# Writing the low parts of weight tiles in pieces of 256 columns on GpSimd

## The chip, the cores and the metric

The kernel runs on one core of one Trainium2 chip. The metric is the device time of one execution in microseconds; smaller is better. The engines are named as in the profile: PE is TensorE (PEld its weight loads), DVE is VectorE, ACT is ScalarE, POOL is GpSimd, SP is SyncE, which issues nearly all DMAs.

## The reference

One layer of a streaming encoder and a final norm, on x of 1024 positions by 1024 channels, all in float32:

```
h = rmsnorm(x) ; proj = h @ w_in          # 4 blocks for a gated DeltaNet, 3 for band attention, 2 branch gates
oa = gated_delta_rule(silu(conv(q)), silu(conv(k)), silu(conv(v)), g, beta)   # 4 heads of 128, chunks of 64
oa = rmsnorm(oa) * silu(z)
ob = chunk_band_attention(qb, kb, vb, rel_bias)                               # 8 heads of 64, band of 9 chunks
mix = sigmoid(ga) * (oa @ w_branch_a) + sigmoid(gb) * (ob @ w_branch_b)
x = x + mix @ w_out
h = rmsnorm(x) ; u = causal_dwconv3(h @ w_up) + b ; gate, up = split(u)
x = x + (silu(gate) * up) @ w_down
return rmsnorm(x)
```

## The kernel before, in words

Every large product is made of three products of a rounded type, float32r, so that float32 accuracy is nearly kept: each operand a is split into a high part `hi` (a rounded copy, made by ACT) and a low part `lo = a - hi` (made by POOL or DVE), and PE adds hi·hi, hi·lo and lo·hi. The function `split` (line 80) issues that pair of instructions; its argument `eng` names the engine of the subtraction, and POOL is taken when it is left out.

`load_w` (line 84) fetches one weight tile of 128 x nk x 128 numbers (nk is 8, or 4 for the two branch matrices) by a DMA into `wraw`, and splits it into `whi` and `wlo`. All three lie in a pool with two buffers each: a new `wraw` is loaded when the tile two before it has been subtracted (SP waits there for POOL), and a new `whi` is written when PE has done with the tile two before it. `proj_half` (line 118) then multiplies one half (512 positions) of the activations `BH` and `BL` with the tile: for each k three matmuls of 512 columns, into the PSUM tile `psph`, of which there are two. DVE or ACT must read one of these before PE can start the next but one.

The stages, in the order of time in the profile:

- to 40 us: first loads, first norm. Weight tiles are split by DVE here.
- 40 to 435 us: the four DeltaNet heads. While PE multiplies projections (`psph`), a chain of small operations runs beside it at high priority: `gdn_prep` and `gdn_prep2` (decay masks `gsh`, `gsl` on POOL, `nL` by DVE and then POOL line 476), a round trip through DRAM (`dL`, then `Lr`), a triangular solve on DVE (`solve_step`: a product, line 516, and a sum, line 518, thirty times), `gdn_apply`, and `gdn_chain` (the state recurrence: `psws`, `U`, `pss`, `S`). The convolution of a projection is three DVE operations (`acc`, line 387) and one more (line 395).
- 435 to 735 us: band attention, two heads at a time, woven with the projections of the next two heads or with the branch gates. DVE makes the low parts of q and k there (`Q` line 787, `Kl` line 797, both from the SBUF tile `u`), scores (`Sb`), the softmax's scaling (line 861) and the low part of the transposed weights (`PTl`, line 877), for which PE waits.
- 735 to 830 us: the two branches are merged (`oh`, `ol`, `bh`, `bl`, weight tiles with nk = 4).
- 830 to 935 us: the output projection (`psout`) and the second norm, with a few splits of activations (`XT1l`, `XT3l`) on POOL.
- 935 us on: the feed-forward part. Its splits are written without `split` (their line is 1165), some 300 us of POOL's time.

The order of the instructions on each engine up to 935 us is set by a list scheduler in the tile framework, from the order of the program, from priorities and from its own estimate of each operation's duration; it is fixed when the program is built. From then on the order is pinned to the program's.

Of the kernel before, what the change touches and what calls it, by code (L numbers as in the profile page):

```python
# [8 lines left out]
F32 = mybir.dt.float32  # L9
F32R = mybir.dt.float32r  # L10
AF = mybir.ActivationFunctionType
ALU = mybir.AluOpType
# [34 lines left out]
def hybrid_kernel(ctx: ExitStack, tc: tile.TileContext, a):  # L47
    nc = tc.nc
# [30 lines left out]

    def split(src, hi, lo, eng=None):  # L80
        nc.scalar.copy(hi, src)  # L81
        (eng or nc.gpsimd).tensor_tensor(out=lo, in0=src, in1=hi.bitcast(F32), op=ALU.subtract)  # L82

    def load_w(src, eng=None):
        nk = src.shape[1]
        raw = wst.tile([P, nk, P], F32, tag="raw", name="wraw")
        nc.sync.dma_start(raw, src)
        hi = wst.tile([P, nk, P], F32R, tag="hi", name="whi")
        lo = wst.tile([P, nk, P], F32R, tag="lo", name="wlo")
        split(raw, hi, lo, eng)  # L90
        return hi, lo
# [155 lines left out]
    def first_w(k0, k1):  # L247
        k = slice(k0, k1)
        nc.sync.dma_start(wraw[:, k], a["w_tiles"][GH][:, k])
        split(wraw[:, k], whi[:, k], wlo[:, k], nc.vector)  # L250
# [18 lines left out]
    wraw, whi, wlo = (gw.tile([P, KT, P], dt, tag=tg, name="wv") for dt, tg in ((F32, "kf"), (F32R, "nKs"), (F32R, "Vs")))  # L269
    nc.sync.dma_start(wraw, a["w_tiles"][2 * GH])  # L270
    split(wraw, whi, wlo, nc.vector)
    ws.append((whi, wlo))
    first_split(1, 2)
# [1540 lines left out]
```

## Time and profile before

| | us |
|---|---|
| runs of the kernel | 1572.12, 1569.9, 1572.11; median 1572.11 |
| span of the profiled execution, first to last instruction | 1571.7 |
| PE busy | 1520.5 (97% of the span) |
| DVE busy | 1122.3 (71%) |
| ACT busy | 715.4 (46%) |
| POOL busy | 597.3 (38%), 455 instructions |
| subtractions of `split` for weight tiles on POOL | 57, of which 41 have 1024 columns and 16 have 512 |

The profiled execution is known by its span; that lies 0.4 us under the median of the runs, so its terms can be set against the median as they stand. In the rows of a timeline the first two numbers are the start and the duration in us, `xN` is a merged series of N instructions, and a bracket gives the idle time of that engine just before, and whose end it waited for.

### The profile page before, as it was taken

How to read it: one execution, taken by the hardware profiler on the slowest of the kernel's cores; microseconds unless marked ns; L12 is line 12 of the kernel's file. 1: busy time of each engine (PE TensorE's matmuls, PEld its weight loads, DVE VectorE, ACT ScalarE, POOL GpSimd, SP SyncE). 2: the span in 40 equal slices, each digit the busy share in tenths (PEclk: the TensorE clock that was granted, in tenths of full speed). 3: DMA queues.
4: the chain of work that ended last, by engine and by line, in shares of the span. 5: the costliest groups of instructions: out<-in, count | busy, mean ns of one | idle time of the engine just before them, and what ended most of it. 6: DMA issues, size and time to landing. Idle time of an engine off the chain costs nothing.

```text
span 1571.7 us, 21185 instructions
## 1 busy us (share of the span) xinstructions
PE 1520.5 (97%) x7687; PEld 1246.0 (79%) x7687; DVE 1122.3 (71%) x2146; ACT 715.4 (46%) x1408; POOL 597.3 (38%) x455
## 2 busy tenths in 40 slices
PE   8999999999999999999999999999999999999997
PEld 6778777886777788787887888888888888788875
DVE  7885867948536878866664567777777777786886
ACT  7644526363225656654222345444444443433344
POOL 3522223212131101110220259877777775323253
PEclk9999999999999999999999999999999999999998
DMA  8112131122131101113553213323223232775523
GB/s 297 40 45 88 44 101 31 54 78 68 61 125 49 36 23 57 30 61 119 171 180 109 94 67 107 122 101 101 101 101 101 101 101 98 264 233 162 180 81 141
DMA packets 74505, 162.03 MB, mean 103 GB/s; under 512 B 15649, under 2 KB 16929, under 8 KB 74401
## 3 DMA queue, kind: packets, MB, share of 16 engines
q1 hardware_dynamic: 74400, 160.68, 30.8%
q8 instruction: 60, 0.98, 0.2%
q14 instruction: 45, 0.36, 0.1%
HBM read 120.55 MB, written 40.11 MB: 102 GB/s over the span
## 4 chain that ended last, share of the span: by engine, by line
PE 49%; DVE 3%; issue 2%; DMA 1%; ACT 1%; SPq 1%; POOL 0%; POOLq 0%; DVEq 0%; ACTq 0%
PE psph L52 8%; PE pb L52 7%; PE psd L52 6%; PE psout L52 5%; PE pa L52 5%; PE pc L52 5%; PE pb L1151 4%; PE psd L1506 3%; PE pa L1151 2%; PE pc L1151 2%; DVE wdl L1165 1%; DVE yu L1165 1%; PE pso L52 1%; SPq L1165 1%; DMA araw<-dA 1%
## 5 line engine op out<-in xcount | busy, mean ns | idle before, releaser
L82 POOL TENSOR_TENSOR wlo<-wraw,whi 128x1024 fp32r<-128x1024 f32 (+1 forms) x57 | 120.0, 2106 | 477.8 <-ACT whi L81 288.1
L52 PE MATMUL psph<-BH,whi 128*128 128x512 f32 x688 | 280.7, 408 | 10.5 <-ACT BH L220 5.2
L52 PE MATMUL psph<-BL,whi 128*128 128x512 f32 x688 | 275.6, 401 | 1.2 <-DVE BL L221 1.2
L52 PE MATMUL psph<-BH,wlo 128*128 128x512 f32 x688 | 275.3, 400 | 0.0
L52 PEld LDWEIGHTS psph<-BH,whi 128*128 128x128 f32 x688 | 130.6, 190 | 33.4 <-ACT BH L220 5.4
L1165 POOL TENSOR_TENSOR ol<-wraw,oh 128x512 fp32r<-128x512 f32 x110 | 150.4, 1385 | 6.6 <-ACT oh L1165 6.5
L52 PEld LDWEIGHTS psph<-BL,whi 128*128 128x128 f32 x688 | 130.7, 190 | 22.9 <-DVE BL L221 2.2
L52 PEld LDWEIGHTS psph<-BH,wlo 128*128 128x128 f32 x688 | 130.4, 190 | 22.9
L52 PE MATMUL psd<-wdl,ah 128*128 128x512 f32 (+1 forms) x311 | 121.9, 392 | 5.3 <-DVE wdl L1165 5.3
L1165 POOL TENSOR_TENSOR al<-araw,ah 128x1024 fp32r<-128x1024 f32 (+1 forms) x28 | 68.3, 2441 | 145.8 <-ACT ah L1165 145.7
L52 PE MATMUL psd<-wdh,ah 128*128 128x512 f32 (+1 forms) x311 | 120.2, 390 | 1.5 <-ACT wdh L1165 1.5
L1506 PE MATMUL psd<-wdh,al 128*128 128x512 f32 (+1 forms) x311 | 121.0, 389 | 0.0
L1165 POOL TENSOR_TENSOR wraw<-wraw 128x512 f32<-128x512 f32 x86 | 119.1, 1385 | 4.9
L1165 ACT CAST oh<-wraw 128x512 fp32r<-128x512 f32 x110 | 67.8, 619 | 103.5 <-POOL wraw L1165 103.3
L1165 DVE TENSOR_TENSOR wdl<-W,wdh 128x512 fp32r<-128x512 f32 x77 | 86.6, 1163 | 27.9 <-ACT wdh L1165 27.9
L1165 ACT CAST ah<-araw 128x1024 fp32r<-128x1024 f32 (+1 forms) x39 | 40.6, 1040 | 113.0 <-PE psd L52 57.8
L81 ACT CAST whi<-wraw 128x1024 fp32r<-128x1024 f32 (+2 forms) x61 | 55.3, 907 | 73.0 <-PE psph L52 50.3
L1165 POOL TENSOR_TENSOR gl<-wraw,gh 128x512 fp32r<-128x512 f32 x42 | 56.2, 1340 | 68.6 <-ACT gh L1165 68.6
L52 PEld LDWEIGHTS psd<-wdl,ah 128*128 128x128 f32 x311 | 58.7, 189 | 19.8 <-DVE wdl L1165 8.0
L52 PEld LDWEIGHTS psd<-wdh,ah 128*128 128x128 f32 x311 | 58.8, 189 | 14.1 <-ACT wdh L1165 1.9
L1151 PE MATMUL pa<-BH,gh 128*128 128x512 f32 x176 | 68.6, 390 | 0.0
L52 PE MATMUL pa<-BH,gl 128*128 128x512 f32 x176 | 68.5, 389 | 0.0
(343 smaller groups left out, 3851.0 us busy)
## 6 DMA issues: line engine op xcount, KB each, us to landing
wraw<-w_up SPq DMA_DIRECT2D x44, 512.0 KB, 5.1
wraw<-w_tiles SPq DMA_DIRECT2D x42, 512.0 KB, 3.5
araw<-dA SPq DMA_DIRECT2D x77, 256.0 KB, 3.0
dA<-yu SPq DMA_DIRECT2D x33, 512.0 KB, 3.1
W<-w_down SPq DMA_DIRECT2D x44, 256.0 KB, 4.9
xt<-x SPq DMA_DIRECT2D x16, 512.0 KB, 5.1
dG<-gt SPq DMA_DIRECT2D x16, 512.0 KB, 2.9
ta<-dG SPq DMA_DIRECT2D x16, 256.0 KB, 2.8
```

What stands on the lines that cost most here:

```text
L52: last["mm"] = nc.tensor.matmul(*args, **kw).ins
L81: nc.scalar.copy(hi, src)
L82: (eng or nc.gpsimd).tensor_tensor(out=lo, in0=src, in1=hi.bitcast(F32), op=ALU.subtract)
L1151: i = nc.tensor.matmul(ps, wh[:, k], xh[:, k], start=start and k == 0, stop=False, **kw)
L1165: return lambda *args, **kw: tc.keep_in_program_order(f(*args, **kw))
L1506: i = nc.tensor.matmul(ps, al[:, j, ts], wh[:, es], start=False, stop=stop, **kw)
```

## The change

Where `split` is called without an engine and the source has three dimensions with an even middle one, the subtraction is written as a loop over pairs of that dimension. For a weight tile a pair is 2 x 128 = 256 columns: four instructions take the place of one of 1024, and two that of one of 512. The copy on ACT stays whole. The condition also holds for `XT1l` and `XT3l` (4 x 128: two pieces), and for `glo`, the low part of the log decays (8 x 4 columns: four pieces of 8).

```
     def split(src, hi, lo, eng=None):
         nc.scalar.copy(hi, src)
+        if eng is None and len(src.shape) == 3 and src.shape[1] % 2 == 0:
+            for k in range(0, src.shape[1], 2):
+                nc.gpsimd.tensor_tensor(out=lo[:, k:k + 2], in0=src[:, k:k + 2], in1=hi.bitcast(F32)[:, k:k + 2],
+                                        op=ALU.subtract)
+            return
         (eng or nc.gpsimd).tensor_tensor(out=lo, in0=src, in1=hi.bitcast(F32), op=ALU.subtract)
```

Lines behind line 82 move down by five. On POOL, in the second DeltaNet head's preparation (around 72 to 87 us), the program read before (a bracket names whose semaphores an instruction waits for):

```order
L461 TENSOR_TENSOR mb<-ngt_608,nb 128x512
L82 TENSOR_TENSOR wlo<-wraw,whi 128x1024 [waits DMAHW0_49,PE_49,Activation_49]
L417 TENSOR_TENSOR gsh<-cn,ghi 128x512 [waits PE_49]
L418 TENSOR_TENSOR gsl<-cn,glo 128x512 [waits PE_49]
L476 TENSOR_TENSOR nL<-nL,mb 128x512 [waits DVE_49,Pool_49]
```

and reads now:

```order
L466 TENSOR_TENSOR mb<-ngt_611,nb 128x512
L84 TENSOR_TENSOR wlo<-wraw,whi 128x256 [waits DMAHW0_49,PE_49,Activation_49]
L84 TENSOR_TENSOR wlo<-wraw,whi 128x256 x3
L422 TENSOR_TENSOR gsh<-cn,ghi 128x512 [waits PE_49]
L423 TENSOR_TENSOR gsl<-cn,glo 128x512 [waits PE_49]
L481 TENSOR_TENSOR nL<-nL,mb 128x512 [waits DVE_49,Pool_49]
```

The four pieces stand in the place of the one instruction; the first carries its waits, the other three none, and `nL` still comes behind them all. PE waits for POOL at the first `wlo` matmul of a tile as before, and now also at the first matmul of each later piece: 311 of its rows wait for POOL instead of 175.

Elsewhere hardly anything moves. DVE and SP keep their order, and PE and ACT are changed in two places of the DeltaNet stage. The larger is on ACT near 138 us, where `gdn_apply` of one head (`U`) meets `gdn_prep` of the next (`nKs`, `jk`); before:

```order
L559 COPY WQ<-psW 128x4x64 x2
L436 COPY nKs<-psk 128x512
L438 ACTIVATE jk,ssk<-nKs 128x128
L563 COPY U<-psU 128x512
L438 ACTIVATE jk,ssk<-nKs 128x128
L436 COPY nKs<-psk 128x512
L438 ACTIVATE jk,ssk<-nKs 128x128 x2
L81 CAST whi<-wraw 128x1024
```

and now:

```order
L564 COPY WQ<-psW 128x4x64 x2
L568 COPY U<-psU 128x512
L441 COPY nKs<-psk 128x512 x2
L443 ACTIVATE jk,ssk<-nKs 128x128 x2
L81 CAST whi<-wraw 128x1024
```

The copy of `U` goes ahead of both copies of `nKs`, and the next `whi` comes behind two of the squares `jk` instead of four.

## The prediction

> **What bounds the kernel now.** I read the page first, for the engine that fills the span and for what the touched group costs:
>
> ```profile
> span 1571.7 us, 21185 instructions
> PE 1520.5 (97%) x7687; PEld 1246.0 (79%) x7687; DVE 1122.3 (71%) x2146; ACT 715.4 (46%) x1408; POOL 597.3 (38%) x455
> L52 PE MATMUL psph<-BH,wlo 128*128 128x512 f32 x688 | 275.3, 400 | 0.0
> ```
>
> PE is the bound, with 51 us of idle time in all. So the change can gain only what it takes out of those 51 us, and can lose wherever it adds to them. The third row is the first surprise: the matmuls that read `wlo` had no idle time before them, so PE never waits for POOL's subtraction. Making a low part ready sooner is worth nothing by itself.
>
> Next I asked whom PE waits for (total us, times, longest):
>
> ```profile
> PE pss L52 <- DVE U L579: 7.3, 6, 1.6
> PE psp L872 <- DVE PTl L877: 5.7, 5, 1.8
> PE psp L872 <- DVE ast L860: 3.2, 3, 1.1
> PE psph L52 <- DVE gt L171: 3.1, 3, 1.8
> PE psws L52 <- DVE S L584: 1.9, 2, 1.6
> PE psp L872 <- DVE Sb L861: 1.7, 1, 1.7
> PE psph L52 <- DVE u L381: 1.0, 1, 1.0
> PE pso L52 <- DVE PTl L877: 0.5, 1, 0.5
> PE psph L52 <- DVE u L778: 1.2, 2, 0.9
> ```
>
> The first eight groups, 24.4 us, are all waits for DVE in the DeltaNet and attention stages. DVE is busy 71% of the span: it is not slow on average, it is late at a few places. The timeline around one of them shows why:
>
> ```profile
> 531.05 2.41 POOL L82 TENSOR_TENSOR wlo<-wraw,whi 128x1024 fp32r<-128x1024 f32 x1 [26.75 <-PE psp L872]
> 531.57 3.15 DVE L787 SCALAR_TENSOR_TENSOR Q<-u,Q 64x512 fp32r<-64x512 f32 x2
> 535.43 0.76 PE L872 MATMUL psp<-ident,Sb 128*128 128x128 f32 x5 [1.79 <-DVE PTl L877]
> ```
>
> Two `Q` operations should take 1.4 us and took 3.15: the first began at 531.57 while POOL ran (531.05 to 533.46), and ended 0.54 us after POOL did. Both of its tensor inputs lie in SBUF. A DVE operation of that kind stands still until POOL's instruction is over; one with a PSUM input runs through. Going over all DVE rows before 935 us that are longer than others of their form, I find the same at nearly every long `wlo`, and 16 of PE's idle gaps, 21.5 of the 24.4 us, come within four us behind such a held operation: eight in the DeltaNet stage (0.99, 1.84, 1.07, 1.64, 1.60, 1.30, 1.07, 1.20 = 10.7) and eight in attention (1.69; 1.79, 1.77, 1.79; three of 1.08; 0.48 = 10.8). What POOL costs here is the length of its longest instruction, not its sum.
>
> **The change part by part.** *The price of a piece.* No instruction of 256 columns is in the trace. The forms that are (count, busy, mean ns):
>
> ```profile
> L82 POOL TENSOR_TENSOR wlo<-wraw,whi 128x1024 fp32r<-128x1024 f32 x41 | 99.4, 2425 | 383.4 <-ACT whi L81 210.0 <-PE psp L872 173.4
> L82 POOL TENSOR_TENSOR wlo<-wraw,whi 128x512 fp32r<-128x512 f32 x16 | 20.6, 1290 | 94.4 <-ACT whi L81 78.1 <-PE psp L872 16.3
> L441 POOL TENSOR_TENSOR bv<-beta,rk 128x8 f32<-128x8 f32 x4 | 1.3, 313 | 0.3
> ```
>
> The slope is (2425 - 1290)/512 = 2.22 ns a column, so 256 columns are 1290 - 568 = 722 ns. From below a piece is a quarter of the long one, 606 ns; from above, the 8-column operation as its fixed part, 313 + 550 = 0.86 us. I take 0.72, the line through the two rows of this very operation. Added to POOL: 41 x (4 x 722 - 2425) = 19.0 us, 16 x (2 x 722 - 1290) = 2.5, the six activation splits about 0.9, `glo` under 1: 23 us more, and 148 more instructions, all beside PE's work (its 0.0 us of idle above). So the fixed part of an instruction, 155 ns by the line through the two rows, costs nothing here. The Trainium skill's "VectorE: DVE Perf Modes" (the section on the TRN2 errata) advises tiles of 512 elements and more on VectorE and ScalarE, because each instruction pays a fixed latency; if that held for this engine and POOL's 23 us lay on the path, the sum would be 1595.
>
> *Does DVE get in between the pieces?* On this all depends, and the trace has cases of POOL instructions that follow each other at once while DVE stands waiting:
>
> ```profile
> 1023.31 1.29 POOL L1165 TENSOR_TENSOR gl<-wraw,gh 128x512 fp32r<-128x512 f32 x1
> 1024.56 1.73 POOL L1165 TENSOR_TENSOR ol<-wraw,oh 128x512 fp32r<-128x512 f32 x1
> 1023.56 1.58 DVE L1165 TENSOR_TENSOR yu<-yu 128x512 f32<-128x512 f32 x1
> 925.91 2.17 POOL L1165 TENSOR_TENSOR ol<-wraw,oh 128x512 fp32r<-128x512 f32 x1 [0.30 <-ACT oh L1165]
> 928.16 1.62 POOL L1165 TENSOR_TENSOR wraw<-wraw 128x512 f32<-128x512 f32 x1
> 926.87 3.46 DVE L1165 TENSOR_TENSOR gl<-wraw,gh 128x512 fp32r<-128x512 f32 x2
> 65.76 0.70 POOL L82 TENSOR_TENSOR glo<-g,ghi 128x32 fp32r<-128x32 f32 x1
> 65.39 1.75 DVE L387 SCALAR_TENSOR_TENSOR acc<-u,prm,acc 128x512 f32<-128x512 f32 x2 [0.77 <-ACT acc L385]
> ```
>
> At 1024.6 DVE's `yu` runs first and POOL's `ol` is the longer for it by 0.44 us. At 926.9 DVE has two in a row: the first goes at 928.08, then POOL's `wraw`, which had been waiting, and only then the second. So they take turns, by who asked first. In both cases POOL's second instruction waited for a semaphore of its own; the pieces two to four carry no wait. The one case without is `glo`, which took 0.70 us because DVE's first `acc` (65.39, over at 66.35) got in ahead of it.
>
> *What the gaps become.* I replay the DVE rows behind each hold with pieces of 0.72 us from POOL's recorded start, taking turns. At 531.05: piece one ends 531.77, the first `Q` goes and ends 532.3, piece two runs to 533.05, the second `Q` ends 533.6. It ended 534.72, so DVE is 1.1 us early, and of the 1.79 us about 1.0 is recovered. Where the held operation is alone, the whole 1.7 us come back (257.25: 1.64); where DVE has a row of such operations, each stands still for its own piece and little is left (117.03 in the solve: 0.9 of 1.84; 372.08: 0.5 of 1.07). Recovered in the DeltaNet stage: 0.9 + 1.07 + 1.64 + 0.6 + 0.95 + 0.5 + 0.95 = 6.6; in attention 1.4 + 3 x 1.0 + 3 x 0.5 + 0.2 = 6.1. One gap grows instead, by the way `nL` lies behind the pieces in POOL's order:
>
> ```profile
> 73.04 2.84 POOL L82 TENSOR_TENSOR wlo<-wraw,whi 128x1024 fp32r<-128x1024 f32 x1
> 78.33 1.28 POOL L476 TENSOR_TENSOR nL<-nL,mb 128x512 f32<-128x512 f32 x1
> 79.64 1.82 SPq L481 DMA_DIRECT2D dL<-nL  x4
> 86.68 0.17 DVE L516 TENSOR_TENSOR tmp<-Zt,Lr 128x8 f32<-128x8 f32 x1 [0.85 <-DMA Lr<-dL]
> 91.20 0.50 PE L52 MATMUL psph<-BH,whi 128*128 128x512 f32 x1 [0.99 <-DVE u L381]
> ```
>
> Four pieces with two DVE operations among them end 0.9 us later, `nL`, its DMAs and the first solve step with it, and `acc` and `u` are queued behind that step on DVE: I take 0.4 us more idle for PE. In the other heads `nL` stands ahead of the pieces, or, at 256 us, the first solve step comes long after it:
>
> ```profile
> 256.33 1.74 POOL L476 TENSOR_TENSOR nL<-nL,mb 128x512 f32<-128x512 f32 x1
> 275.56 0.15 DVE L516 TENSOR_TENSOR tmp<-Zt,Lr 128x8 f32<-128x8 f32 x1
> ```
>
> *The 16 tiles of 512 columns.* DVE's `ta` is held by seven of them (0.94 us over its usual 0.69), but PE has no gap there:
>
> ```profile
> 752.42 1.63 DVE L976 TENSOR_TENSOR ta<-ta,tb 128x512 f32<-128x512 f32 x1
> ```
>
>  The first piece is ready at 0.72 instead of 1.29 us, the second at about 2 us with `ta` between, and it is first read 1.36 us (six weight loads) after the first. Cost nothing, gain nothing; the cover is the one matmul group of 2.7 us that runs meanwhile. *The long tiles' own readiness:* the nearest case:
>
> ```profile
> 480.45 2.39 POOL L82 TENSOR_TENSOR wlo<-wraw,whi 128x1024 fp32r<-128x1024 f32 x1 [16.60 <-ACT whi L81]
> 485.44 0.19 PEld L52 LDWEIGHTS psph<-BH,wlo 128*128 128x128 f32 x1
> SPq L87 <- POOL wlo L82: 436.0, 44, 28.2
> ACT whi L81 <- PE psph L52: 50.3, 30, 9.6
> ```
>
> It is 2.6 us early, its first piece will be 4.3 us early. *SP* waits for the last piece before it loads the next `wraw`, 44 times, now 0.5 to 1.4 us longer, with stores and bias loads queued behind; but the tile's next step, `whi`, waits for PE and not for that load, so this is hidden as long as PE is the later one. *The added PE waits,* some 136: those there already stand before matmuls with 0.0 us of idle, so nothing. *The order on ACT and PE near 138 us:* PE has no gap over 0.3 us in the 20 us behind it; nothing, either way under 1 us.
>
> *The sum:* 6.6 + 6.1 - 0.4 = 12.3 us. By pieces of 0.61 it would be about 16.5, by 0.86 about 9. I take off 2 us, since a PE that runs on meets the next late DVE result sooner: 10 us, 1572.1 to 1562. The profile's span of 1571.7 against the median of 1572.1 makes no difference to it.
>
> **The rivals.** *The pieces hold DVE as one.* Pieces two to four wait for nothing; if POOL keeps its grip from one to the next, a hold grows from 2.43 to 2.89 us. At 16 gaps that is 7.4 us: 1579.5, slower. It decides once DVE is let in only after the third piece or later; at the second it still gains. For it speaks that `glo` is one case only, against it that this case went the other way. The Trainium skill's "GPSIMD Engine Reference" (section Instruction dispatch) says that consecutive Pool instructions are no barrier between its cores: a core starts the next instruction when its own share is done. By that rule pieces without waits could overlap and never let go; the row of `glo` does not agree.
>
> *The waits only move.* DVE's held work is conserved where it has many such operations in a row, and behind each closed gap another late result shows. By the dear piece the solve's and three attention gaps already give 0.1 us or less; if the other gaps are half refilled, 3 us remain: 1569, at the edge of what can be told from no change. Against it: attention's gaps over 0.3 us are, all but two near 470 us (`u`, 1.2 us), these eight.
>
> *POOL comes late itself.* If the 0.9 us of the first `nL` happened at all four heads and SP's later loads were seen, 4 x 1 us and a few: 1576. The slack rows speak against it.
>
> **How the numbers follow.** The forecast (turns, 1555 to 1568): 0.74. Waits only move (around 1569, half of it above): 0.12. The pieces hold as one (1576 to 1582): 0.08. POOL late (1572 to 1577): 0.06. A difference of 0.2%, 3.1 us, is about what a measurement of this kernel tells from no change. Faster by more than that: 0.74 and half of 0.12, 0.80; slower: 0.08 and a third of 0.06, 0.10; the rest, 0.10, within it. Range: from 1555 (cheap piece, nothing taken off) to 1572, which leaves out the rivals that end slower and little else.
>
> **What would show it.** The pieces as a row of 196 at 0.7 to 0.8 us, longer where DVE gets in; POOL's busy time 620 to 645; no DVE row of these stages held longer than about 0.8 us; the three waits of PE for `PTl` near 0.8 each instead of 1.8, the 257 us gap gone, and the eight groups together 11 to 14 us. I am wrong if DVE rows stand still over two and more pieces, or if PE's idle time before 735 us has only changed its names.

## The result, and the profile after

| | median us | lowest to highest | runs | ratio to before, 95% interval |
|---|---|---|---|---|
| before | 1571.01 | 1569.78 to 1572.12 | 4 | |
| changed | 1555.69 | 1554.61 to 1559.45 | 4 | 0.9901 [0.9888, 0.9914] |

The change makes the kernel 15.3 us faster, by the interval 13.5 to 17.6. I had said 10 us, 1562, with a range from 1555 to 1572: the result lies inside it, but close to its lower end. The page's totals after:

```profile
span 1553.3 us, 21372 instructions
PE 1518.1 (98%) x7687; PEld 1245.5 (80%) x7687; DVE 1091.1 (70%) x2146; ACT 716.3 (46%) x1408; POOL 639.3 (41%) x603
```

The touched group among POOL's groups by line and shape (count, busy, mean ns of one, then idle time before them):

```profile
L84 POOL TENSOR_TENSOR wlo<-wraw,whi 128x256 fp32r<-128x256 f32 x196 | 157.1, 831 | 442.0 <-ACT whi L81 262.8 <-PE psp L877 165.9 <-PE pss L52 7.1
```

POOL works 42 us longer, and PE waits for that at one place only (`nL`, below). DVE's busy time falls by 31 us although it has the same 2146 instructions: what is counted as busy before held much standing still. PE's idle time, span less busy, goes from 51.2 to 35.2 us, so 16.0 of the 18.4 us of span come from there. PE's waits after (total us, times, longest), with the two that are now largest ahead of the groups known from before:

```profile
PE psd L52 <- DVE wdl L1170: 5.6, 6, 1.7
PE psph L52 <- ACT BH L225: 5.5, 1, 5.5
PE pss L52 <- DVE U L584: 3.1, 5, 1.2
PE psp L877 <- DVE PTl L882: 1.8, 4, 0.5
PE psp L877 <- DVE ast L865: 1.6, 3, 0.7
...
PE psph L52 <- DVE u L386: 1.4, 1, 1.4
PE psph L52 <- DVE u L783: 1.2, 2, 0.9
PE psws L52 <- DVE S L589: 1.1, 3, 0.5
PE psp L877 <- DVE Sb L866: 0.8, 1, 0.8
```

The eight groups that I had added up, 24.4 us, are down to 10.0 (the eighth, `pso` for `PTl`, has 0.2; the one for `gt` is gone). The place that the prediction replayed, two `Q` operations beside a weight tile's low part, looks like this in the timeline now:

```profile
518.72 3.72 POOL L84 TENSOR_TENSOR wlo<-wraw,whi 128x256 fp32r<-128x256 f32 x4 [26.26 <-PE psp L877]
519.24 1.91 DVE L792 SCALAR_TENSOR_TENSOR Q<-u,Q 64x512 fp32r<-64x512 f32 x2
521.86 0.77 PE L877 MATMUL psp<-ident,Sb 128*128 128x128 f32 x5 [0.54 <-DVE PTl L882]
```

The two `Q` take 1.91 us instead of 3.15, the four pieces 3.72 instead of 4 x 0.72, and PE waits 0.54 instead of 1.79 us: DVE gets in between the pieces.

For the experiments I cut the span at the first matmul of each stage and add up, within each, the stretches without a matmul (length / idle, us). The idle time of the last stage goes to its last matmul. The stages left out, a short one of 19.0 us between the two and merge to feed-forward (92.7, 95.0, 418.3), are the same in all within 0.5 us. Two things in the lengths are not the edits'. From the first matmul of DeltaNet to that of `psba` near 13 us, before any piece on POOL, the 14 traces take 6.7 to 8.5 us, before being the longest (8.5, changed 6.9), in part by a wait for `BL` (the view of waits before):

```profile
PE psph L52 <- DVE BL L221: 1.2, 1, 1.2
```

The trace of e3, which has pieces, has that wait too (1.14 us), the changed kernel's has not; so 1.6 us of the 11.8 us by which DeltaNet is shorter, and 1.2 of its 10.2 us of idle time, come from the start of these two executions and not from the change. And stretches at half the granted clock, of which more below, cost 6.8 us of DeltaNet in e2, 3.4 in e3, 1.7 each in e6 and e7, and 3.4 us of attention in e2; the other entries of these two columns have none.

| kernel | DeltaNet | attention | last stage |
|---|---|---|---|
| before | 460.6 / 16.4 | 250.2 / 11.1 | 230.7 / 6.8 |
| changed (pieces of 256) | 448.8 / 6.2 | 244.0 / 4.6 | 230.0 / 7.1 |
| e2: long one and pieces | 476.2 / 25.3 | 262.7 / 18.0 | 229.9 / 6.9 |
| e3: pieces of 128 | 453.2 / 7.8 | 243.9 / 3.6 | 231.6 / 7.2 |
| e4: pieces of 512 | 453.2 / 9.7 | 249.0 / 9.9 | 231.2 / 7.1 |
| e5: pieces in DeltaNet alone | 449.3 / 6.9 | 250.1 / 11.1 | 230.5 / 6.6 |
| e6: long ones on DVE | 449.9 / 8.0 | 239.6 / 0.6 | 230.5 / 7.4 |
| e7: `al` in pieces too | 450.9 / 6.9 | 243.9 / 4.6 | 225.5 / 2.5 |
| e8: `nL` on DVE | 446.5 / 6.1 | 243.9 / 4.6 | 233.2 / 7.4 |
| e10: each stage's best form | 447.9 / 6.2 | 239.6 / 0.5 | 223.7 / 2.6 |

### The profile page after: what moved, and what is told of

Read it like the earlier page. It is cut to its first block, busy times and chain, and to the rows that moved or that the text cites. A ratio compares the mean times of both kernels' runs of the same rounds, so it can differ in the third digit from the quotient of the medians.

```text
span 1553.3 us, 21372 instructions
## 1 busy us (share of the span) xinstructions
PE 1518.1 (98%) x7687; PEld 1245.5 (80%) x7687; DVE 1091.1 (70%) x2146; ACT 716.3 (46%) x1408; POOL 639.3 (41%) x603
## 4 chain that ended last, share of the span: by engine, by line
PE 49%; DVE 3%; issue 2%; DMA 1%; ACT 1%; SPq 1%; POOL 0%; POOLq 0%; DVEq 0%; ACTq 0%
PE psph L52 8%; PE pb L52 7%; PE psd L52 6%; PE psout L52 5%; PE pa L52 5%; PE pc L52 5%; PE pb L1156 4%; PE psd L1511 3%; PE pa L1156 3%; PE pc L1156 2%; DVE wdl L1170 1%; DVE yu L1170 1%; PE pso L52 1%; SPq L1170 1%; DMA araw<-dA 1%
## 5 line engine op out<-in xcount | busy, mean ns | idle before, releaser
L84 POOL TENSOR_TENSOR wlo<-wraw,whi 128x256 fp32r<-128x256 f32 x196 | 157.1, 831 | 442.0 <-ACT whi L81 262.8
L1170 DVE TENSOR_TENSOR wdl<-W,wdh 128x512 fp32r<-128x512 f32 x77 | 88.9, 1192 | 28.1 <-ACT wdh L1170 28.1
```

Of the source, the lines that this page charges most:

```text
L84: nc.gpsimd.tensor_tensor(out=lo[:, k:k + 2], in0=src[:, k:k + 2], in1=hi.bitcast(F32)[:, k:k + 2], op=ALU.subtract)
L1170: return lambda *args, **kw: tc.keep_in_program_order(f(*args, **kw))
```

## The experiments

The theory: DVE operations with two SBUF inputs stand still for one POOL instruction at a time, so what counts is the length of a POOL instruction, not the sum, nor when a tile is ready. The rivals: readiness counts; POOL's load or number of instructions counts; or what is won is lost again behind the next late result. Each experiment changes one thing, but for e12 and the last three, which join edits.

**Readiness (e1_reversed).** The pieces in reverse order, so that the columns that PE reads first are ready last:

```
-            for k in range(0, src.shape[1], 2):
+            for k in reversed(range(0, src.shape[1], 2)):
```

> The pieces of 256 columns are written in reverse order, so PE's first matmul of a tile waits for the last piece. Theory (a two-input DVE operation stands still for one POOL instruction, and pieces shorten that): the holds are as in the change, 1554 to 1558 us. Rival (the gain comes from low parts that are ready sooner): the readiness is worse than before, 1570 us or more.

Measured: 1556.43 us, ratio to before 0.9905 [0.9889, 0.9922], the changed kernel's within the interval. Readiness of the first piece is worth nothing.

**The long instruction back, ahead of the pieces (e2_long_and_pieces).** For the tiles of 1024 columns the whole subtraction runs first, and then the four pieces write the same numbers again:

```
         if eng is None and len(src.shape) == 3 and src.shape[1] % 2 == 0:
+            if src.shape[1] * src.shape[2] == 1024:
+                nc.gpsimd.tensor_tensor(out=lo, in0=src, in1=hi.bitcast(F32), op=ALU.subtract)
             for k in range(0, src.shape[1], 2):
```

> In front of the four pieces of each tile of 1024 columns the one long instruction is issued as well, with the same result; the 512-column tiles are in pieces. Theory (length of the longest POOL instruction): the long holds of 2.4 us are back and the pieces add some, the eight groups of PE's waits for DVE are at 24 us or more, 1570 to 1578 us. Rival (what counts is how many pieces or waits there are, or the changed order near 138 us): close to the change, 1555 to 1560 us.

Measured: 1604.67 us, ratio 1.0213 [1.019, 1.0235]. The direction is the theory's, the size is not: 27 us above the upper end of what I had expected. Its timeline shows the pieces hold DVE again behind the long one, at the same place in attention, and the first late `nL` with PE's wait behind it:

```profile
548.80 2.40 POOL L84 TENSOR_TENSOR wlo<-wraw,whi 128x1024 fp32r<-128x1024 f32 x1 [25.17 <-ACT whi L81]
551.28 3.58 POOL L86 TENSOR_TENSOR wlo<-wraw,whi 128x256 fp32r<-128x256 f32 x4
549.32 3.56 DVE L794 SCALAR_TENSOR_TENSOR Q<-u,Q 64x512 fp32r<-64x512 f32 x2
83.54 1.29 POOL L483 TENSOR_TENSOR nL<-nL,mb 128x512 f32<-128x512 f32 x1
94.39 0.50 PE L52 MATMUL psph<-BH,whi 128*128 128x512 f32 x1 [3.45 <-DVE u L388]
```

The `Q` pair takes 3.56 us, more than before's 3.15. `nL` starts at 83.54 instead of 78.33, and the wait for `u` becomes 3.45 us. The two stages' idle time grows by 15.9 us against before, but their length by 28.1. The rest is the clock, by a table of stretches (the stretch, its length, busy time and count of PE, PEld, DVE, ACT and POOL, granted clock, DMA share, GB/s):

```profile
94.00:98.00 4.00, 3.61 (x10) 2.86 (x11) 3.92 (x9) 1.31 (x2) 1.93 (x3) 0.64 0.00 0
```

Behind that stall PE runs at half the clock for some 3.4 us. Such stretches stand at six places of these two stages, five of them behind stalls: six times 1.7 us are 10 of the 12 us left. So POOL's load does count once it is large enough to make `nL` late, by 0.4 us in the changed kernel and by 2.5 us here, and this run has both, long holds and a fuller POOL: it does not price the holds alone.

**The size of a piece (e4_pieces_512, e3_pieces_128).** Two pieces of 512, or eight of 128:

```
-            for k in range(0, src.shape[1], 2):
-                nc.gpsimd.tensor_tensor(out=lo[:, k:k + 2], in0=src[:, k:k + 2], in1=hi.bitcast(F32)[:, k:k + 2],
+            for k in range(0, src.shape[1], 4):        # e4 (middle dimension a multiple of 4); e3: every k, k + 1
+                nc.gpsimd.tensor_tensor(out=lo[:, k:k + 4], in0=src[:, k:k + 4], in1=hi.bitcast(F32)[:, k:k + 4],
```

> Pieces of 512 columns, two for a long tile, one for a short one. Theory by the same replay: 4.2 us recovered, 1567 us. Rival (half of the change's gain, by half of its cuts): 1563 us.

> Pieces of 128 columns, eight for a long tile, each about 0.44 to 0.5 us. Theory: replaying the rows of before with such pieces gives 18.5 to 19.7 us instead of the 13.3 of pieces of 256, so 5 to 6 us less than the change: about 1550 us, POOL's busy time up by 15 to 25 us. Rival (the fixed part of an instruction and the turns with DVE eat it): 1555 us or more.

Measured: 512 columns 1565.18 us, ratio 0.9961 [0.9946, 0.9976], about halfway between theory and rival, so that the time does not part the two and the rows must; 128 columns 1560.31 us, 0.9922 [0.9904, 0.9939], 10 us above what I expected and on the rival's side. The timeline of the `Q` pair with pieces of 512:

```profile
523.17 2.98 POOL L84 TENSOR_TENSOR wlo<-wraw,whi 128x512 fp32r<-128x512 f32 x2 [26.55 <-PE psp L877]
523.68 3.01 DVE L792 SCALAR_TENSOR_TENSOR Q<-u,Q 64x512 fp32r<-64x512 f32 x2
```

Each of the two `Q` stands still for a piece of its own, and the pair is hardly sooner done than before (3.01 against 3.15); so attention gains 1.2 us only, and DeltaNet, where more of the held operations stand alone, 7.4 (1.3 of them at the start). This is the turn-taking of the prediction, seen where it hurts. With 128 columns the `Q` rows are held still less (groups by line and shape, whose second number behind the bar is the mean ns of one). The changed kernel:

```profile
L792 DVE SCALAR_TENSOR_TENSOR Q<-u,Q 64x512 fp32r<-64x512 f32 x16 | 13.1, 816 | 1.6 <-ACT Q L791 1.2
```

Pieces of 128:

```profile
L792 DVE SCALAR_TENSOR_TENSOR Q<-u,Q 64x512 fp32r<-64x512 f32 x16 | 12.5, 783 | 1.6 <-ACT Q L791 1.2
L84 POOL TENSOR_TENSOR wlo<-wraw,whi 128x128 fp32r<-128x128 f32 x392 | 198.3, 541 | 417.7 <-ACT whi L81 236.8 <-PE psp L877 160.3 <-PE pss L52 20.6
```

and its timeline and then its table of stretches:

```profile
90.36 0.50 PE L52 MATMUL psph<-BH,whi 128*128 128x512 f32 x1 [1.98 <-DVE u L386]
```

```profile
90.50:95.00 4.50, 4.50 (x13) 3.55 (x14) 4.35 (x13) 1.84 (x3) 0.10 (x1) 0.62 0.12 47
350.50:354.50 4.00, 3.92 (x14) 3.44 (x15) 2.28 (x7) 1.45 (x3) 0.00 (x0) 0.57 0.00 0
```

Attention's idle time does fall, by 1.0 us. But POOL has 42 us more to do than with pieces of 256, the wait behind the late `nL` grows from 1.43 to 1.98 us, another at 350.6 us from 1.20 to 1.81, and behind both the clock is granted at half for 3.4 us. My expectation had neither. The counter-test takes `nL` out of POOL's queue:

```
-        nc.gpsimd.tensor_tensor(out=nL, in0=nL, in1=mb, op=ALU.mult)
+        nc.vector.tensor_tensor(out=nL, in0=nL, in1=mb, op=ALU.mult)
```

> Pieces of 128 columns (as in e3_pieces_128), and nL's second multiplication on VectorE. Theory: pieces of 128 hold VectorE back still less (13.3 us in all against 20.8 with 256, up to 720 us), and e3 lost that again because GpSimd's queue, 41 us fuller, made the first head's nL late: a stall of 1.98 us at 90.4 us and 3.4 us at half clock behind it (1.7 us). Without nL in that queue both go: 1560.3 less 3.7 = 1556.6 us, range 1555 to 1558. Rival (finer pieces cost in many other places, by order or by VectorE and GpSimd taking turns oftener): 1559 to 1561.

Measured (e12): 1556.75 us, ratio 0.9906 [0.9885, 0.9926], as the theory said; both long stalls are gone from its trace. Of the three sizes 256 is the best here: shorter pieces hold DVE less, but cost POOL more in all, and that makes `nL` late. Even without that they gain nothing over 256 columns: e8 below, with the same `nL`, takes 1555.78 us.

**Are the two stages' gains independent? (e5_deltanet_only).** Pieces up to the attention part, whole instructions from there:

```
+    pieces = [True]
     def split(src, hi, lo, eng=None):
-        if eng is None and len(src.shape) == 3 and src.shape[1] % 2 == 0:
+        if pieces[0] and eng is None and len(src.shape) == 3 and src.shape[1] % 2 == 0:
...
+    pieces[0] = False                     # ahead of the attention part
```

> Pieces only in the DeltaNet part; from the attention part on, the low parts are again one instruction each. Theory (each held-back row gives its own stall, and the stalls of the two parts are independent): DeltaNet keeps the 448.8 us that it has with pieces everywhere (460.6 before), attention is back at 250.2 us (244.0 with pieces), so 1555.7 + 6.2 = 1562 us, range 1560.5 to 1564, and a held-back Q, PTl or Kl row of over 1 us is there again in attention alone. Rival (what is won in one part is partly given back in the other, because transfers and weight tiles run ahead or behind): 1557 to 1559, or over 1565.

Measured: 1562.08 us, ratio 0.9931 [0.9916, 0.9946]. DeltaNet keeps its 449.3 us and attention is back at 250.1, with the waits for `PTl` of 1.8 us. So some 10 us of the gain come from DeltaNet (11.3 by the table, 1.2 of them at the start; 10.9 by the medians) and 6 from attention, and neither is given back later.

**The long tiles taken off POOL (e6_long_on_dve).** DVE makes the 41 long low parts itself:

```
-        split(raw, hi, lo, eng)
+        split(raw, hi, lo, nc.vector if nk == KT else eng)
```

> The 41 low parts of 1024 columns are made by VectorE itself, as one instruction each; GpSimd keeps the low parts of 512 columns, in pieces. Theory (what cost the time was VectorE held for the length of one GpSimd instruction, up to 2.4 us): nothing holds VectorE for over 0.9 us, but each low part now stands in VectorE's own row for about 1.2 us, longer than a piece of 0.7 and shorter than the long one of 2.4; so between the two kernels: 1560 us, range 1556 to 1566. Rival (what counts is VectorE's total time, which goes up by some 50 us): slower than before, over 1572. Rival (GpSimd's load counts, which falls by some 130 us): under 1555.

Measured: 1552.57 us, ratio 0.9872 [0.9857, 0.9887], better than I expected and than the pieces. The new group of DVE, by line and shape:

```profile
L87 DVE TENSOR_TENSOR wlo<-wraw,whi 128x1024 fp32r<-128x1024 f32 x42 | 52.0, 1237 | 4.2 <-ACT whi L81 4.0
```

The timeline of the `Q` pair, and PE's largest wait in the first solve:

```profile
518.96 1.40 DVE L792 SCALAR_TENSOR_TENSOR Q<-u,Q 64x512 fp32r<-64x512 f32 x2
524.06 1.21 DVE L87 TENSOR_TENSOR wlo<-wraw,whi 128x1024 fp32r<-128x1024 f32 x1
```

```profile
PE psph L52 <- DVE Zt L523: 3.1, 1, 3.1
```

DVE has some 51 us more of its own (41 of 1237 ns) and is busy 1112.6 us in all, less than in the kernel before. My mistake was to treat the 1.2 us as a hold at the same place: its `whi` is there at 518.32, but the order of the program puts the instruction at 524.06, behind `Q` and the next `PTl`, for which PE waits, whereas a POOL instruction of these traces starts when its own inputs allow and falls on whatever DVE is doing. Attention's idle time is 0.6 us. In DeltaNet one stall of 3.1 us in the first solve takes the place of several. POOL's load falls too, from 639.3 to 512.4 us, and the rival that counts it had forecast such a time, under 1555, where the theory's range began at 1556; this run alone does not part the two. The changed kernel against e6 does for DeltaNet: POOL is busy 145 us there against 62, and PE's idle time is less (6.2 against 8.0). So it does against before: POOL is busier in both stages (145 against 124 us, 42 against 30), and PE is idle for 15.5 us less even without the wait for `BL`.

**The same remedy in the last stage (e7_al_pieces).** The changed kernel left 5.6 us of waits for `wdl`, after DVE rows beside `al`, 1024 columns on POOL:

```
-        (V if k % 2 and plan[2 * k // FH][0] in ("P5", "P6", "P7", "P4") else G).tensor_tensor(
-            out=al[:, 0:n], in0=raw[:, 0:n], in1=ah.bitcast(F32)[:, 0:n], op=ALU.subtract)
+        if k % 2 and plan[2 * k // FH][0] in ("P5", "P6", "P7", "P4"):
+            V.tensor_tensor(out=al[:, 0:n], in0=raw[:, 0:n], in1=ah.bitcast(F32)[:, 0:n], op=ALU.subtract)
+        else:
+            for j in range(2 * n):
+                q = (slice(0, P), j // 2, slice(j % 2 * 256, j % 2 * 256 + 256))
+                G.tensor_tensor(out=al[q], in0=raw[q], in1=ah.bitcast(F32)[q], op=ALU.subtract)
```

> The changed kernel, and the low part of the activations in the last stage (al, 1024 columns on GpSimd) in pieces of 256 as well. Theory: the same holding back is there (the wdl rows of VectorE take 2.5 to 2.9 us beside an al instead of 0.7, and TensorE waits 5.6 us for wdl in 6 places, up to 1.72 us); with pieces the waits for wdl fall to 1 to 3 us and the time to 1552 us, range 1551 to 1554.5. Rival (the last stage is set by the arrival of its weight blocks or by ScalarE's high parts, and the wdl wait is taken over by those): 1555.7 within 1 us.

Measured: 1550.75 us, ratio 0.9853 [0.9836, 0.9871]. The timeline at one place of the changed kernel:

```profile
1353.39 2.39 POOL L1170 TENSOR_TENSOR al<-araw,ah 128x1024 fp32r<-128x1024 f32 x1 [7.31 <-ACT ah L1170]
1353.86 3.07 DVE L1170 TENSOR_TENSOR wdl<-W,wdh 128x512 fp32r<-128x512 f32 x2 [2.19 <-ACT wdh L1170]
1356.38 0.50 PE L52 MATMUL psd<-wdl,ah 128*128 128x512 f32 x1 [1.25 <-DVE wdl L1170]
```

The same place with `al` in pieces, and PE's waits in that stage:

```profile
1353.94 3.03 POOL L1170 TENSOR_TENSOR al<-araw,ah 128x256 fp32r<-128x256 f32 x3 [5.19 <-ACT ah L1170]
1354.41 1.96 DVE L1170 TENSOR_TENSOR wdl<-W,wdh 128x512 fp32r<-128x512 f32 x2 [1.33 <-ACT wdh L1170]
```

```profile
PE psd L52 <- ACT wdh L1170: 2.1, 1, 2.1
PE psd L52 <- DVE wdl L1170: 0.3, 1, 0.3
```

The wait for `wdh` grows from 1.5 to 2.1 us, so a little of what is won goes the rival's way. The mechanism is not one of weight tiles: here too DVE reads two SBUF inputs beside a long POOL instruction, PE waits for the result, and pieces give time back, 4.5 us of the last stage.

**The first head's `nL` (e8_nl_on_dve).** The edit of e12, made to the changed kernel:

> The changed kernel, and the second multiplication of nL (128x512, 1.4 us on GpSimd, behind four pieces in its queue) made by VectorE. Theory: the 1.43 us stall at 88.8 us comes from nL, its transfers and Lr being later than before; without GpSimd's queue ahead of it nL is there 1.5 to 3 us earlier and the stall falls to 0.3 to 1 us: 1555 us, range 1553.5 to 1555.7. Rival (the transfers dL and Lr set that time, or VectorE's own four extra instructions make other results later): 1555.7 to 1557.

Measured: 1555.78 us, ratio 0.9889 [0.9874, 0.9903]; no change against the changed kernel. The rival's words fit half of it: the stall at 88.8 us is gone, as the theory had it, and DeltaNet is 2.3 us shorter, but new waits for `S`, six of up to 1.1 us, stand in the waits, and the table of stretches has the clock:

```profile
1450.00:1553.00 103.00, 90.61 (x390) 73.55 (x389) 78.80 (x95) 43.23 (x74) 38.57 (x22) 0.95 0.37 123
```

In the profiled execution the last stage has the clock at 0.95 where the changed kernel had 0.99, and is 3.2 us longer with hardly more idle time. Most likely that is not the edit's: both traces have the same two waits there (1.54 us for `wdh`, then 0.9 for `wdl`), but they fall differently into the clock's windows of 3.41 us (last section). In e8 1.83 us of the idle time lie in one window and half clock follows, in the changed kernel 1.43 and 0.98 us in two. The other three runs have no trace.

**Put together (e9_long_dve_al, e10_mixed, e11_long_dve_al_nl).** e9 joins the edits of e6 and e7, e11 adds `nL` on DVE; e10 keeps pieces on POOL in DeltaNet, takes DVE for long low parts from attention on, and has `al` in pieces and `nL` on DVE:

```
-        split(raw, hi, lo, eng)
+        split(raw, hi, lo, nc.vector if nk == KT and not pieces[0] else eng)
```

> The 41 long low parts on VectorE (as in e6_long_on_dve) and al in pieces on GpSimd (as in e7_al_pieces). Theory (the stalls of the stages are independent, so the gains add): e6's 1552.6 less the 4.9 us that e7 gained against the changed kernel = 1547.6 us, range 1546 to 1550. Rival (an earlier start or a lower clock in the last stage takes some of it back): 1550 to 1553.

> Each stage in the form that did best there: DeltaNet with pieces on GpSimd and nL's second multiplication on VectorE (446.5 us in e8_nl_on_dve), from the attention part on the long low parts on VectorE (239.6 us in e6_long_on_dve), al in pieces in the last stage (225.5 us in e7_al_pieces). Theory (independent stages): 5.3 + 446.5 + 19.0 + 239.6 + 92.7 + 95.0 + 418.3 + 225.5 = 1541.9 us of span, 1543.7 us as a run, range 1542 to 1547. Rival (what one stage gains is partly taken back by the next or by a half-clock stretch behind one longer stall): 1547 to 1551.

> As e9_long_dve_al, and nL's second multiplication on VectorE as well. Theory: the 3.06 us stall at 95.8 us and the 3.4 us at half clock behind it (worth 1.7 us) belong to the first head's solve steps behind other VectorE work there; nL 0.7 to 1.5 us earlier shortens that stall to 1.5 to 2.5 us and with luck spares the half clock: 1545 us, range 1543.5 to 1548. Rival (Lr's arrival sets it, not nL's multiplication): 1547.6, as e9.

Measured: e9 1545.34 us, 0.9825 [0.9809, 0.9841], a little below its range; e10 1544.26, 0.9819 [0.9803, 0.9834]; e11 1550.11, 0.9853 [0.9832, 0.9874]. e10 has the lowest time, 28 us under before and 11 under the change, though it cannot be told from e9; its span comes out as the sum said (1541.6 against 1541.9), DeltaNet being 1.4 us longer than its term and the last stage 1.8 shorter. Its totals, and PE's largest wait:

```profile
span 1541.6 us, 21376 instructions
PE 1515.2 (98%) x7687; PEld 1244.9 (81%) x7687; DVE 1076.4 (70%) x2166; ACT 716.0 (46%) x1408; POOL 618.3 (40%) x617
```

```profile
PE psph L52 <- ACT BH L227: 5.8, 2, 5.2
```

PE is idle for 26 us now, and the start (`BH`) is its longest wait. e11 missed, but not by the stall: that falls from 2.85 us in e9 to 1.97, as expected. DeltaNet takes 453.3 us with 7.9 idle, and the trace has the clock at half from 54.5 to 57.9 and from 133.0 to 139.8 us, which takes 5.1 us; without that it would be 448.2, and e9's DeltaNet, 450.4 with 1.7 us lost in the same way, 448.7. All four runs of e11 have a lower mean clock (0.994 to 0.996) than those of e9 (0.997 to 0.998). No single stall over 0.8 us stands just before these two stretches; why the clock goes down there stays open.

## Why the prediction was right, and where its sizes were off

*What bounds the kernel* was read rightly: PE, held up by late DVE results that come behind a held operation. e4, e6 and e7 show it: where the held rows get shorter, or go, PE's waits behind them do too.

*The price of a piece*, 0.72 us: the median of the 722 to 1253 ns seen is 742 ns; the mean of 831 has DVE's turns in it, as the prediction said it would. POOL's busy time of 639.3 lies in 620 to 645, near its upper end (42 us more where I had added up 23). The holds left on DVE in these stages last up to 0.9 us, where I had said 0.8; the longest stand beside POOL instructions of 512 columns that the change leaves whole (`mb`, `gsh`, `gsl`).

*Turns between pieces that wait for nothing* was the step on which all depended, and it held, as at `glo`. The Trainium skill's "SBUF — State Buffer" (section Who interferes with whom) says that a VectorE instruction with two SBUF inputs contends with a GpSimd instruction that reads SBUF, calls the shared pair of ports an exclusive lock, and has issue order decide who blocks; the `Q` rows agree, 3.15 us beside one of 1024, 3.01 beside two of 512, 1.91 beside four of 256.

*The sum* was too small: 12.3 less 2 against 18.4 us between the two spans. Attention's term was right (6.1, and its idle time fell by 6.5; the eight groups of waits came to 10.0 us, where I had 11 to 14). The step that was mis-sized is DeltaNet's, 6.2 net, where idle time fell by 9.0 without the wait for `BL` at the start. Two places in DeltaNet make up the difference, and the 2 us taken off the whole sum were a third error:

- I left out a stall, since the view of waits names no engine for it but "issue". It is of the same kind: a held `acc`, ahead on DVE of the chain that ends in `g`, for which `psdec` waits. The timeline before:

```profile
41.72 2.89 DVE L387 SCALAR_TENSOR_TENSOR acc<-u,prm,acc 128x512 f32<-128x512 f32 x1
61.10 0.19 DVE L326 TENSOR_TENSOR g<-lnu,prm 128x32 f32<-128x32 f32 x1
61.40 0.38 PE L52 MATMUL psdec<-g,cm 128*128 128x32 f32 x2 [1.42 <-issue]
```

and after:

```profile
40.44 1.23 DVE L392 SCALAR_TENSOR_TENSOR acc<-u,prm,acc 128x512 f32<-128x512 f32 x1
58.31 0.19 DVE L331 TENSOR_TENSOR g<-lnu,prm 128x32 f32<-128x32 f32 x1
58.61 0.38 PE L52 MATMUL psdec<-g,cm 128*128 128x32 f32 x2
```

  `g` is 2.8 us sooner, 1.3 of them because this execution started faster (`acc` itself is that much earlier), and the 1.42 us are gone; with pieces of 512 they are still 1.3, and in e2 1.8.
- In the solve I took back 0.9 of the 1.84 us at 117.03, thinking that each step would stand still for a piece of its own. All of it went (and at 275.68 1.16 of 1.60, where I had 0.6). One step before, in the timeline:

```profile
111.09 2.31 DVE L516 TENSOR_TENSOR tmp<-Zt,Lr 128x152 f32<-128x152 f32 x1
```

  and the steps beside the four pieces after:

```profile
108.14 3.09 POOL L84 TENSOR_TENSOR wlo<-wraw,whi 128x256 fp32r<-128x256 f32 x4 [6.00 <-ACT whi L81]
108.62 0.43 DVE L521 TENSOR_TENSOR tmp<-Zt,Lr 128x160 f32<-128x160 f32 x1
109.45 0.39 DVE L521 TENSOR_TENSOR tmp<-Zt,Lr 128x168 f32<-128x168 f32 x1
```

  Between two products a step has a sum with one input of 0.33 us, which is not held, and the pieces fell mostly on that: a product of usually 0.33 takes 0.4 us.
- Of the 2 us for the next late result little was needed: the one new gap over 0.3 us in DeltaNet has 0.45 us, and attention has none.

The 0.4 us for the late `nL` came out as 0.44 (0.99 before, 1.43 in the timeline now), by luck as to the size: against the start of the tile's subtraction, 2.5 us earlier than before (70.53), the pieces end 0.9 us later, as I had it, but `nL` ends 1.9 later, being held itself (1.74 us instead of 1.28).

```profile
77.22 1.74 POOL L481 TENSOR_TENSOR nL<-nL,mb 128x512 f32<-128x512 f32 x1
88.83 0.50 PE L52 MATMUL psph<-BH,whi 128*128 128x512 f32 x1 [1.43 <-DVE u L386]
```

Part of the 18.4 us is the profiled execution itself: a run's time lies 1.8 us above its span (1555.1 for 1553.3), so the span of 1571.7 belongs to an execution of about 1573.5, and my remark that the difference to the median was nothing was 1.4 us off. By medians the gain is 15.3, and the forecast was right in its mechanism and its direction, and too small by a third.

*The rivals.* That the pieces hold DVE as one is refuted by the `Q` rows. That the waits only move is refuted by PE's idle time, 16.0 us less in all, and by e5, where neither stage gives back what the other wins. That POOL comes late is true at one place in the changed kernel, and costs more with pieces of 128 and in e2. The changed order on ACT and PE near 138 us does nothing that the traces show: PE waits nowhere between 118 and 160 us for more than 0.21 us, before or after.

## What to carry to other kernels

When DVE is not full but late, look at what POOL runs at that moment: the length of one POOL instruction, not POOL's load, is what a DVE operation with two SBUF inputs can lose, once for each such operation in a row. Cut the POOL instruction to about the length of the DVE operations beside it; cutting further gained nothing here, and pushed back what is queued behind on POOL; or give the work to DVE itself, where the order of the program can place it behind what PE waits for. A wait that the profile calls "issue" may be the same thing one chain further away.

## What the runs showed that I had not expected

A stall of PE can cost more than its length. Behind the stalls of 1.98 and 1.81 us in e3 the granted clock was 0.5 for 3.4 us, which costs another 1.7 us each; the run of e3 with the highest mean clock (0.999) took 1555.35 us, the other three (0.995 to 0.996) 1560.2 to 1560.9. It does not follow from the length alone: before's stall of 1.84 us at 117 us left the clock whole. Where a stall lies decides too. In each of the 14 traces all changes of the granted clock fall on one grid of 3.41 us. The 1.98 us of e3 lie in a single window of that grid, in which PE is busy for 1.44 us (stretches of e3):

```profile
87.90:91.31 3.41, 1.44 (x7) 0.88 (x6) 3.33 (x9) 0.92 (x2) 0.48 (x2) 1.00 0.50 154
```

The 1.84 us of the kernel before are cut by an edge of its grid, 0.48 us in one window and 1.36 in the next:

```profile
112.25:115.67 3.42, 2.94 (x13) 2.08 (x12) 3.18 (x8) 0.00 (x0) 0.97 (x1) 1.00 0.00 0
115.67:119.08 3.41, 2.05 (x9) 1.69 (x10) 3.24 (x10) 0.80 (x2) 0.00 (x0) 1.00 0.19 73
```

Over the windows of all traces from 20 us to the last matmul that had the clock whole: 13 held 1.89 us or more without a matmul, and half clock followed on every one; 57 held 1.2 to 1.88 us, and it followed on 8; 135 held 0.6 to 1.2 us, and it followed on none. Of the some 6000 with less it followed on 5, four of them at 51 to 54 us in e2, e7, e11 and e12 and one at 130 us in e11, and for these the traces show no reason. The grid begins at another place in each of the traces, so the same stall can cost the clock in one and not in the next.

The Trainium skill's "TensorE: Matmul & The Clock Gate" (Part 1, What's actually happening) has half clock after an idle window of about 3.4 us, in windows that run freely. The grid agrees; here a window with 1.9 us of idle time in it was enough.
